# A 32-byte shift of the left-side pools, spread row pitches for split weights, and one value buffer less, in an encoder layer on one core

## The chip, the cores and the metric

The kernel runs on one NeuronCore of a Trainium2 chip. The metric is the device time of one launch in microseconds, the median of the runs shown.

## The reference

One layer of an encoder is computed for two sequences of 1024 tokens with a model width of 1024. Each sequence has its own conditioning vector, from which six shifts, scales and gates are made. An input projection feeds a latent attention with four heads and, beside it, a Fourier mixing; one output projection joins them. Behind it stands a SwiGLU feed-forward of width 2816. All values are float32.

```python
h2 = rmsnorm(x, g_ffn) * (1.0 + sc2) + sh2
ffn = (jax.nn.silu(h2 @ w_gate) * (h2 @ w_up)) @ w_down
return x + ga2 * ffn          # then a final rmsnorm with g_final
```

The change touches the feed-forward alone, and by its shift of addresses all that lies on the left side of the on-chip memory.

## The kernel before

**Split products.** A float32 product is made of three matmuls in the type float32r. `split(hi, lo, src)` makes two tiles: ScalarE casts src to hi (line 62) and VectorE subtracts hi from src to make lo (line 63). `mm3(out, lh, ll, rh, rl, ...)` then issues three matmuls of 128x512 on TensorE (lines 78, 79 and 80): lh with rh, lh with rl, ll with rh. In each, the operand that is loaded into the array comes first, and the one that streams through it second.

**Block products.** Each large product of the feed-forward (gate and up, then down) is done with seven products of half-size blocks instead of eight, on sums and differences of blocks. The sums and differences are formed by `sums_w`, `comb_h`, `down_combos` and `put_s`, mostly on GpSimd (lines 134 and 137 are the helpers `sub` and `add`).

**Gate and up.** For each sequence s the loop runs over 22 column blocks of the two weight matrices. The seven combinations of the hidden input, H[k], are held on chip for the whole loop as split pairs of tiles (128 partitions, four chunks of 512). The weights of a block come by DMA into `rgu` (line 1205), are combined, and each of the seven results (128 by 512) is split by `hl` into a tile wh and a tile wl. `prod(ps, k, wt, first)` goes over four chunks c: it loads columns 128c to 128c+127 of wh or wl into the array and streams chunk c of H[k] through it, twelve matmuls for a product. `step(j, ...)` calls prod and then splits the j-th weight of the next block. VectorE and ScalarE take the seven results out of PSUM and form the blocks that GpSimd and SP store to `s_d`.

**Down.** For each sequence seven calls of `prod2` follow: k = 0, 5, 1, 6, 4, 3, 2, into the PSUM banks X, Y, X, Y, Z, Y, Z. Each goes over eleven blocks f. A block's two raw operands are loaded on SP's queue into `draw` (lines 1397 and 1398), which has two buffers of two blocks each; both operands are split by `hl`, and twelve matmuls follow, in which 128 columns of the first operand (ah, al) are loaded and all 512 columns of the second (bh, bl) stream. Between the blocks `hooks` works through a list of small tasks. `resid` loads a piece of the residual into a value buffer (line 1411, SP's queue), multiplies by the gate on VectorE (line 1412) and adds on GpSimd; `first_squares` writes squares into a scratch value buffer on ScalarE (line 1422); `last_part` and `rows_out` finish rows and store them. In the last sequence the seventh product is replaced by a loop over operands that are kept as H tiles (`held`).

**Buffers.** `val()` gives one of VALS value buffers of 128x512, `hl` one of eight wh and one of eight wl buffers. A buffer is given again when its last reader is done; the instruction that writes it first waits for that, and what stands behind it in its engine's or queue's order waits too. The order of instructions on each engine is made by a scheduler from the order of the program text and from these buffers.

**Places.** On-chip memory is filled by pools from two sides. The pool const is the first on the left. Among the left-side tiles are H, rgu, draw and the attention's latents; wh, wl, val, the tables of the projection and the probabilities lie on the right side.

Of the kernel before, what the change touches and what calls it, by code (L numbers as in the profile page):

```python
# [12 lines left out]
F32 = mybir.dt.float32  # L13
F32R = mybir.dt.float32r
# [7 lines left out]
P = 128  # L22
# [10 lines left out]
G = 8  # L33
GD = 64
NOUT = 6
VALS = 18
FF = 2816
NF = FF // P
EPS = 1e-6
# [13 lines left out]
def hybrid_encoder_kernel(ctx: ExitStack, tc: tile.TileContext, a: dict):  # L53
# [7 lines left out]
    def split(hi, lo, src):  # L61
        here["a"] = nc.scalar.copy(hi, src).ins  # L62
        here["v"] = nc.vector.tensor_tensor(out=lo, in0=src, in1=rd(hi), op=ALU.subtract).ins  # L63
# [13 lines left out]
    def mm3(out, lh, ll, rh, rl, first, last, cont=False):  # L77
        nc.tensor.matmul(out, lh, rh, start=first, stop=False, skip_group_check=cont)  # L78
        nc.tensor.matmul(out, lh, rl, start=False, stop=False, skip_group_check=cont)  # L79
        nc.tensor.matmul(out, ll, rh, start=False, stop=last, skip_group_check=cont)  # L80

    const = ctx.enter_context(tc.tile_pool(name="const", bufs=1))
# [7 lines left out]
    mhalf = const.tile([P, 2], F32, name="mhalf")  # L90
    nc.gpsimd.memset(mhalf, -0.5)
    cmask = const.tile([P, 7], F32, name="cmask")
    nc.sync.dma_start(cmask, a["cmask"])

    def rstd(ms, n, rest=None):
# [755 lines left out]
    with ExitStack() as st:  # L851
# [145 lines left out]
        for k in range(nit + 4):  # L997
# [7 lines left out]
            if k < nit:  # L1005
                s, b, h, u = items[k]
# [28 lines left out]
    with ExitStack() as st:  # L1035
# [95 lines left out]
        H = {}  # L1131
# [42 lines left out]
        w5 = st.enter_context(tc.tile_pool(name="p5b", bufs=1, side="right", reuse_waits="tile"))  # L1174
# [5 lines left out]
        def val():  # L1180
            return w5.tile([P, 512], F32, tag="v", name="val", bufs=VALS)

        def hl(v):
            h = w5.tile([P, 512], F32R, tag="wh", name="wh", bufs=8)
            if "gf" not in S:
                S["gf"] = w5.tile([P, D], F32, name="gf")
                w5.tile([P, 2, 512], F32, tag="ga", name="tdb", bufs=1)
            l = w5.tile([P, 512], F32R, tag="wl", name="wl", bufs=8)
            split(h, l, v)
            return h, l  # L1190

# [3 lines left out]
        for s in range(2):  # L1195
# [44 lines left out]
            def prod(ps, k, wt, first):  # L1240
                wh, wl = wt
                for c in range(4):
                    cs = slice(c * P, c * P + P)
                    mm3(ps, wh[:, cs], wl[:, cs], H[k][0][:, c, :], H[k][1][:, c, :], first and c == 0, c == 3, not first)

            def store_s(k, fi, v, eng):
                eng.dma_start(s_d[s][k, fi], v)
# [18 lines left out]
            if s == 0:  # L1266
                wts = [hl(w0[i]) for i in range(2)]
                next(prep, None)
                wts += [hl(w0[i]) for i in (2, 3)]
            else:  # L1270
                wts = first_w
            A = {}
            late = None
            for n, f in enumerate(order):
# [10 lines left out]
                def step(j, ps, k, first, src=src):  # L1285
                    prod(ps, k, cur[j], first)
                    if s == 0 and n == 0:
                        if j == 0:
                            cur.extend(hl(v) for v in w0[4:])
                            w0.clear()  # L1290
                            norm3(1, S.pop("jk3").bitcast(BF16))
                        if j < 3:
                            with behind():
                                for _ in range(2):
                                    next(prep, None)
                            return
                        if j == 3:
                            src = S["w1"] = sums_w(src, lambda i: val(), nc.vector)
                        src = S["w1"]
                        for i in ((), (), (), (0, 1), (2, 3), (4,), (5, 6))[j]:  # L1300
                            nxt.append(hl(src[i]))
                    elif src is not None:
                        nxt.append(hl(src[j]))
                    if s == 0 and n == 1 and j == 2:
                        S.pop("w1", None)
                        flip2(3, [S.pop(("xn", 1, 3, u)) for u in range(2)], bank, lambda g: val())
# [80 lines left out]
            def bsrc(k, f):  # L1387
                r1 = slice(f * P, f * P + P)
                r2 = slice((f + NF // 2) * P, (f + NF // 2) * P + P)
                return {0: wd[r1, :512], 1: wd[r2, :512], 2: wd[r2, 512:], 3: t_d[0, f], 4: t_d[1, f], 5: t_d[2, f], 6: t_d[3, f]}[k]  # L1390

            def prod2(ps, k, first, last, hook=None):
                for f in range(NF // 2):
                    if f % 2 == 0:
                        raw2 = w.tile([P, 2, 2, 512], F32, tag=f"X{f // 2 % 2}", name="draw", bufs=1)
                    raw = raw2[:, f % 2]
                    nc.sync.dma_start(raw[:, 0, :], s_d[s][k, f])  # L1397
                    nc.sync.dma_start(raw[:, 1, :], bsrc(k, f))  # L1398
                    ah, al = hl(raw[:, 0, :])
                    bh, bl = hl(raw[:, 1, :])  # L1400
                    for t in range(4):
                        tt = slice(t * P, t * P + P)
                        mm3(ps[t], ah[:, tt], al[:, tt], bh, bl, first and f == 0, last and f == NF // 2 - 1, not first)
                    if hook is not None:
                        hook(f)
# [61 lines left out]
            X = [bank() for _ in range(4)]  # L1467
            Y = [bank() for _ in range(4)]
            prod2(X, 0, True, True)
            p1 = [val() for _ in range(4)]  # L1470
            for t in range(4):
                nc.scalar.copy(p1[t], X[t])
            prod2(Y, 5, True, True, put_next)
            u2 = [val() for _ in range(4)]
            for t in range(4):
                add(u2[t], Y[t], p1[t], nc.vector)
            prod2(X, 1, False, True, put_next)
            c11 = [val() for _ in range(4)]
            for t in range(4):
# [51 lines left out]
            H = Hn  # L1531
# [99 lines left out]
```

## Time and profile before

| | |
|---|---|
| median of 2 runs | 2116.02 us (2114.76 to 2117.27) |
| span of the profiled execution | 2109.8 us |
| mean granted TensorE clock in it | 0.988 |
| TensorE busy | 2033.0 us (96%) |
| VectorE, ScalarE, GpSimd busy | 1414.4, 906.0, 828.6 us |
| DMA | 371.30 MB, mean 176 GB/s |

The span reaches from the first to the last instruction on the core. The time of a run also holds what lies around it: 6.2 us, if the profiled execution is set against the median of the runs. In the profile's rows PE is TensorE's matmuls, PEld its loads, DVE VectorE, ACT ScalarE, POOL GpSimd, and SPq the queue of SP, which issues most DMAs. A row of a group has the line, the engine, the operation, what is written and read, the shape and count; then the busy time in us and the mean of one in ns; then the idle time just before these instructions and what ended it. A row of a window has the stretch and its length, then for PE, PEld, DVE, ACT and POOL the busy time with the count, then the granted clock, the busy share of the DMA engines and GB/s. A row of waits has the total, the number of times and the longest, in us. A row of the timeline has the start and the duration in us.

### The profile page before, as it was taken

To read this page: it belongs to the slowest core of one execution; us is meant where nothing else is said; L and a number is where in the kernel's file an instruction comes from. 1 tells how busy PE (TensorE), PEld (TensorE's weight loads), DVE (VectorE), ACT (ScalarE), POOL (GpSimd) and SP (SyncE) were. 2 spreads that over 40 slices of the span, in tenths; PEclk is the share of its full clock that TensorE was granted. 3 is DMA by queue.
4 is the path that set the end of the run, shared out by engine and by line. 5 is a ranking of instruction groups with operands and counts; after the bars stand their busy time and mean duration, and the time that the engine had idled before them with its cause. 6 is when DMAs were issued, how large, how long until landed. Compare 5 with 4: busy or idle time off the path is not lost. (4 is left out here: it accounts for less than half of the span.)

```text
span 2109.8 us, 28784 instructions
## 1 busy us (share of the span) xinstructions
PE 2033.0 (96%) x10044; PEld 1667.0 (79%) x10044; DVE 1414.4 (67%) x2087; ACT 906.0 (43%) x1763; POOL 828.6 (39%) x1018
## 2 busy tenths in 40 slices
PE   5899998999999999999999999999999999999998
PEld 2788876888888887788888888887788888888886
DVE  2657756766676678777677677777766666566685
ACT  2656534555565555232333346453233333336441
POOL 1455202111311314888778610235544454420142
PEclk8999999999999999999999999999999999999999
DMA  9575765544544455554554578674332232247772
GB/s 368 194 248 190 248 233 197 113 88 91 159 119 118 150 186 211 180 193 169 194 185 166 174 250 270 222 236 164 131 119 90 91 125 95 81 154 280 233 227 99
DMA packets 184254, 371.30 MB, mean 176 GB/s; under 512 B 19052, under 2 KB 58604, under 8 KB 181036
## 3 DMA queue, kind: packets, MB, share of 16 engines
q1 hardware_dynamic: 166252, 314.00, 44.1%
q0 software_dynamic: 17856, 55.45, 8.9%
q8 instruction: 79, 1.29, 0.2%
q14 instruction: 67, 0.55, 0.1%
HBM read 257.38 MB, written 120.39 MB: 179 GB/s over the span
## 5 line engine op out<-in xcount | busy, mean ns | idle before, releaser
L78 PE MATMUL bank<-H,wh 128*128 128x512 f32 x1232 | 489.6, 398 | 7.7 <-ACT val L1311 4.0
L80 PE MATMUL bank<-H,wl 128*128 128x512 f32 x1232 | 488.9, 397 | 1.4 <-DVE wl L63 1.4
L79 PE MATMUL bank<-H,wh 128*128 128x512 f32 x1232 | 489.0, 397 | 0.0
L137 DVE TENSOR_TENSOR val<-bank,val 128x512 f32<-128x512 f32 x244 | 167.1, 690 | 185.7 <-PE bank L80 178.6
L78 PEld LDWEIGHTS bank<-H,wh 128*128 128x128 f32 x1232 | 232.5, 189 | 66.8 <-ACT val L1311 5.4
L80 PEld LDWEIGHTS bank<-H,wl 128*128 128x128 f32 x1232 | 232.5, 189 | 57.9 <-DVE wl L63 1.7
L79 PEld LDWEIGHTS bank<-H,wh 128*128 128x128 f32 x1232 | 232.7, 189 | 56.2
L63 DVE TENSOR_TENSOR wl<-draw,wh 128x512 fp32r<-128x512 f32 x286 | 203.1, 744 | 82.7 <-ACT wh L62 80.7
L62 ACT CAST wh<-draw 128x512 fp32r<-128x512 f32 x286 | 168.8, 619 | 159.0 <-PE bank L79 83.0
L137 POOL TENSOR_TENSOR val<-val 128x512 f32<-128x512 f32 x58 | 82.9, 1438 | 366.3 <-DVE val L1412 187.6
L79 PE MATMUL bank<-wl,wh 128*128 128x512 f32 x572 | 223.8, 391 | 1.6 <-DVE wl L63 1.6
L80 PE MATMUL bank<-wh,wl 128*128 128x512 f32 x572 | 222.7, 389 | 0.0
L78 PE MATMUL bank<-wh 128*128 128x512 f32 x572 | 222.6, 389 | 0.0
L62 ACT CAST wh<-rgu 128x512 fp32r<-128x512 f32 x172 | 106.7, 621 | 269.7 <-PE bank L79 209.5
L62 ACT CAST wh<-val 128x512 fp32r<-128x512 f32 x133 | 82.2, 622 | 280.5 <-PE bank L79 249.1
L63 DVE TENSOR_TENSOR wl<-val,wh 128x512 fp32r<-128x512 f32 x133 | 141.5, 1066 | 85.6 <-ACT wh L62 85.5
L63 DVE TENSOR_TENSOR wl<-rgu,wh 128x512 fp32r<-128x512 f32 x172 | 169.4, 985 | 4.9 <-ACT wh L62 4.8
L134 POOL TENSOR_TENSOR val<-rgu 128x512 f32<-128x512 f32 x84 | 122.8, 1462 | 125.0 <-DMA rgu<-in_wgu_dram 108.8
L79 PEld LDWEIGHTS bank<-wl,wh 128*128 128x128 f32 x572 | 107.4, 188 | 27.3 <-DVE wl L63 5.3
L78 PEld LDWEIGHTS bank<-wh 128*128 128x128 f32 x572 | 107.4, 188 | 22.4
L80 PEld LDWEIGHTS bank<-wh,wl 128*128 128x128 f32 x572 | 107.4, 188 | 22.0
L134 POOL TENSOR_TENSOR val<-val 128x512 f32<-128x512 f32 x89 | 119.4, 1357 | 1.3
(332 smaller groups left out, 4051.2 us busy)
## 6 DMA issues: line engine op xcount, KB each, us to landing
rgu<-in_wgu_dram SPq DMA_DIRECT2D x86, 512.0 KB
draw<-s_d SPq DMA_DIRECT2D x143, 256.0 KB
s_d<-val POOLq DMA_DIRECT2D x88, 256.0 KB, 4.1
draw<-t_d SPq DMA_DIRECT2D x88, 256.0 KB
s_d<-val SPq DMA_DIRECT2D x66, 256.0 KB
draw<-in_w_down_dram SPq DMA_DIRECT2D x55, 256.0 KB
wada<-in_w_ada_dram SPq DMA_DIRECT2D x13, 1024.0 KB
xt<-in_x_dram SPq DMA_DIRECT2D x16, 512.0 KB
```

The lines of the kernel that those rows point to most:

```text
L62: here["a"] = nc.scalar.copy(hi, src).ins
L63: here["v"] = nc.vector.tensor_tensor(out=lo, in0=src, in1=rd(hi), op=ALU.subtract).ins
L78: nc.tensor.matmul(out, lh, rh, start=first, stop=False, skip_group_check=cont)
L79: nc.tensor.matmul(out, lh, rl, start=False, stop=False, skip_group_check=cont)
L80: nc.tensor.matmul(out, ll, rh, start=False, stop=last, skip_group_check=cont)
L134: return eng.tensor_tensor(out=out, in0=x, in1=y, op=ALU.subtract).ins
L137: eng.tensor_tensor(out=out, in0=x, in1=y, op=ALU.add)
```

## The change

A tile of 8 float32 values (32 bytes in each partition) that nothing uses is added to the pool const, so that everything allocated later on the left side lies 32 bytes higher. The tiles wh and wl get room for four rows of 132 and of 134 elements (528 and 536 bytes) in place of 512 elements, and in gate and up the four chunks of 128 columns are written to and loaded from these rows. In down, `hl` is called with flat=True and uses the first 512 elements without gaps, in the same larger buffers. VALS goes from 18 to 17. The lines behind the new tile move by one in the new file, those behind the new code by four.

```diff
-VALS = 18
+VALS = 17
...
     cmask = const.tile([P, 7], F32, name="cmask")
+    const.tile([P, 8], F32, name="phase")
...
-        def hl(v):
-            h = w5.tile([P, 512], F32R, tag="wh", name="wh", bufs=8)
+        def hl(v, flat=False):
+            h = w5.tile([P, 4, 132], F32R, tag="wh", name="wh", bufs=8)
             if "gf" not in S:
                 S["gf"] = w5.tile([P, D], F32, name="gf")
                 w5.tile([P, 2, 512], F32, tag="ga", name="tdb", bufs=1)
-            l = w5.tile([P, 512], F32R, tag="wl", name="wl", bufs=8)
+            l = w5.tile([P, 4, 134], F32R, tag="wl", name="wl", bufs=8)
+            if flat:
+                h, l = (t.rearrange("p a b -> p (a b)")[:, :512] for t in (h, l))
+            else:
+                h, l, v = h[:, :, :128], l[:, :, :128], v.rearrange("p (a b) -> p a b", a=4)
             split(h, l, v)
             return h, l
...
                 for c in range(4):
-                    cs = slice(c * P, c * P + P)
-                    mm3(ps, wh[:, cs], wl[:, cs], H[k][0][:, c, :], H[k][1][:, c, :], first and c == 0, c == 3, not first)
+                    mm3(ps, wh[:, c, :], wl[:, c, :], H[k][0][:, c, :], H[k][1][:, c, :], first and c == 0, c == 3, not first)
...
-                    ah, al = hl(raw[:, 0, :])
-                    bh, bl = hl(raw[:, 1, :])
+                    ah, al = hl(raw[:, 0, :], True)
+                    bh, bl = hl(raw[:, 1, :], True)
```

## The prediction

> **What bounds the kernel now.** I read the page first, for the busy shares:
>
> ```profile
> span 2109.8 us, 28784 instructions
> PE 2033.0 (96%) x10044; PEld 1667.0 (79%) x10044; DVE 1414.4 (67%) x2087; ACT 906.0 (43%) x1763; POOL 828.6 (39%) x1018
> ```
>
> TensorE is busy for 96% of the span, so a gain must come from the pace at which matmuls follow each other, or from its last waits. The groups by line show which matmuls these are, and that they are not equally quick:
>
> ```profile
> L78 PE MATMUL bank<-H,wh 128*128 128x512 f32 x1232 | 489.6, 398 | 7.7 <-ACT val L1311 4.0 <-DVE val L137 3.4 <-ACT wh L62 0.2
> L79 PE MATMUL bank<-H,wh 128*128 128x512 f32 x1232 | 489.0, 397 | 0.0
> L80 PE MATMUL bank<-H,wl 128*128 128x512 f32 x1232 | 488.9, 397 | 1.4 <-DVE wl L63 1.4
> L80 PE MATMUL bank<-wh,wl 128*128 128x512 f32 x572 | 222.7, 389 | 0.0
> L78 PE MATMUL bank<-wh 128*128 128x512 f32 x572 | 222.6, 389 | 0.0
> L78 PE MATMUL bank<-H 128*128 128x512 f32 x44 | 17.1, 389 | 0.0
> ```
>
> The same 128x512 product costs 397 ns with H moving and wh or wl loaded (the gate/up stage, 3696 of them), 389 ns in the down stage (1716), and 389 ns with H moving and H loaded. These are durations of pipelined instructions; the pace is a count over a stretch. The windows are, in order: gate/up of sequence 0, gate/up of sequence 1, two stretches of down, and the last products, where both operands are H tiles.
>
> ```profile
> 1000.00:1140.00 140.00, 140.00 (x601) 112.70 (x601) 98.43 (x101) 43.01 (x72) 108.38 (x100) 1.00 0.52 179
> 1560.00:1830.00 270.00, 270.00 (x1159) 217.37 (x1158) 169.01 (x192) 81.95 (x138) 130.63 (x112) 1.00 0.28 98
> 1240.00:1380.00 140.00, 140.00 (x620) 115.95 (x619) 103.85 (x148) 75.89 (x138) 24.59 (x22) 1.00 0.78 259
> 1960.00:2030.00 70.00, 70.00 (x311) 57.97 (x310) 48.28 (x66) 30.55 (x57) 19.25 (x16) 1.00 0.68 222
> 2072.00:2095.00 23.00, 23.00 (x103) 19.02 (x103) 14.37 (x23) 2.90 (x8) 10.20 (x35) 1.00 0.35 129
> ```
>
> A window counts each matmul that it touches, 1.7 more than it starts (0.39 us over the pace). So the paces are 140/599.3 = 233.6 and 270/1157.3 = 233.3 ns in gate/up, 140/618.3 = 226.4 and 70/309.3 = 226.3 ns in down, and 23/101.3 = 227.0 ns in the last products. The granted clock is 1.00 in all five. Load elsewhere does not explain the 7 ns: GpSimd is busy 77% in the first row and 48% in the second, at one pace, and the down rows carry more DMA (0.78, 0.68) than the slow ones (0.52, 0.28). What goes with it is where the operands lie. In the built program H lies at 0 modulo 64 bytes and wh and wl at 32, so moving and loaded operand differ by 32. In down both are wh or wl (both 32), and in the last products both are H (both 0): offset 0. The waits of TensorE in these stages are small:
>
> ```profile
> PE bank L78 <- ACT val L1311: 4.0, 2, 2.6
> PE bank L78 <- DVE val L137: 3.4, 3, 2.1
> PE bank L79 <- DVE wl L63: 1.6, 3, 1.0
> PE bank L80 <- DVE wl L63: 1.4, 1, 1.4
> ```
>
> 10.4 us of waiting in 1300: pace is the bound, and the feeding chains are just in time.
>
> **The change, part by part.** No matmul is added or removed; the built programs have the same TensorE order. What changes is addresses and one buffer.
>
> *Gate/up.* H moves to 32 modulo 64. With rows of 528 bytes, the four 128-column chunks of a wh tile start 0, 16, 32 and 48 bytes from H; those of wl, at 536 bytes, 0, 24, 48 and 8, or 32, 56, 16 and 40 in every second buffer, since a wl buffer of 2144 bytes is 33.5 times 64. So the shift alone would give offset 0 everywhere, and the pitches spread the offsets again. Nothing in the trace runs at these offsets in full; the nearest is the stage of wm, where operands lie at 0, 8, 32 and 40 from each other in turn. From its first to its last row here are 35 intervals:
>
> ```profile
> 317.77 0.39 PE L80 MATMUL bank<-wm,A 128*128 128x512 f32 x1
> ...
> 325.90 0.40 PE L78 MATMUL bank<-wm,B 128*128 128x512 f32 x1
> ```
>
> 8.13/35 = 232.3 ns: a mixture is nearly as slow as 32 throughout. I take 232.3 against 233.4 as the mean of the two gate/up stages: -1.1 x 3696 = -4 us. Bounds: every pair at the down pace, -7 x 3696 = -26 us; a second step of the same size up, +26 us. If the whole fixed cost of a load beside a stream went away, the gain would be larger. That cost comes from the 256-wide products:
>
> ```profile
> 340.53 0.28 PE L80 MATMUL gb<-ql,wq_l 128*128 128x256 f32 x1
> ...
> 341.59 0.28 PE L80 MATMUL gb<-wq_h,ql 128*128 128x256 f32 x1
> ```
>
> Nine intervals give 117.8 ns; 2 x (226.4 - 117.8) = 217.2 ns is the streaming of 512 columns, and 233.4 - 217.2 = 16.2 ns x 3696 = 60 us is the floor. The Trainium skill, "TensorE: Matmul & The Clock Gate", Back-to-back issue gap, has about 216 ns for 512 columns alone, by which it would be 64 us.
>
> *Attention.* The latents are left-side tiles and also move by 32. Half of their 640 products now run at offset 32 and come to 0, as the mean of these rows, between 389 and 397, bears out:
>
> ```profile
> L906 PE MATMUL ps_s<-lat,qp 128*128 128x512 f32 x128 | 50.6, 396 | 0.0
> L907 PE MATMUL ps_s<-lat,qp 128*128 128x512 f32 x128 | 50.6, 395 | 0.0
> L79 PE MATMUL gb<-pt,ckv 128*128 128x256 f32 x256 | 72.7, 284 | 0.0
> L79 PE MATMUL gb<-ql,wq_h 128*128 128x256 f32 x64 | 18.3, 286 | 0.0
> ```
>
> 320 x 7 = 2.2, taken as -2 us (0 to -4.5). The 768 products of pt with ckv go the other way, from 32 to 0, where the ql row is 2 ns longer: +1 us (-1.5 to +4).
>
> *Down.* Here hl is asked for flat tiles, so no chunk is spread, but the wl buffers still alternate between 0 and 32. A pair of calls takes neighbouring buffers, so al and bl now always differ by 32. Of each three products (ah with bh, ah with bl, al with bh) the one that streams bl while al is loaded has offset 32. If that one alone pays: 572 x 7 = +4 us; all three: 1716 x 7 = +12; none: 0. I take +5, since the next product starts later too.
>
> *The splits.* Cast and subtraction now write four runs of 128 with a gap. The nearest row is L873, which writes four runs of 64:
>
> ```profile
> L873 DVE TENSOR_TENSOR qsk<-qt,qsk 128x256 fp32r<-128x256 f32 x16 | 8.9, 559 | 1.8 <-ACT qsk L872 1.1
> L867 DVE TENSOR_TENSOR qt<-gb,rc 128x256 f32<-128x256 f32 x16 | 6.6, 415 | 1.1 <-PE gb L80 1.1
> L63 DVE TENSOR_TENSOR wl<-rgu,wh 128x512 fp32r<-128x512 f32 x172 | 169.4, 985 | 4.9 <-ACT wh L62 4.8
> ```
>
> At worst 559/415 = 1.35 times 985 ns, 0.35 us more per twelve products (2.8 us). VectorE is busy 70% and 63% in the gate/up windows, and would reach 82%: hidden, 0. Without that cover it would be 305 x 0.35 = 107 us.
>
> *Seventeen value buffers.* The order of instructions stays the same on all engines but around the fifth and sixth product of down (Z with k = 4, Y with k = 3), so only there do values run out: p1, u2, c11 and u3 hold sixteen, and the residual loads (L1411) and the scratch of the squares (L1422) share the rest: two before, one after. A load waits in SP's queue for a free buffer, and the draw loads behind it wait too. Before, two loads are in flight and the additions that free them come in pairs:
>
> ```profile
> 2007.49 3.21 SPq L1411 DMA_DIRECT2D val<-x_d  x2
> ...
> 2020.87 0.82 SPq L1411 DMA_DIRECT2D val<-x_d  x2
> 2021.79 0.37 SPq L1397 DMA_DIRECT2D draw<-s_d  x1
> 2022.21 0.43 SPq L1398 DMA_DIRECT2D draw<-t_d  x1
> 2025.06 2.02 SPq L1411 DMA_DIRECT2D val<-x_d  x2
> ```
>
> ```profile
> 2011.86 3.52 POOL L137 TENSOR_TENSOR val<-val 128x512 f32<-128x512 f32 x2 [1.06 <-DMA val<-x_d]
> 2023.59 3.15 POOL L137 TENSOR_TENSOR val<-val 128x512 f32<-128x512 f32 x2 [1.44 <-DMA val<-x_d]
> 2050.56 1.61 POOL L137 TENSOR_TENSOR val<-val 128x512 f32<-128x512 f32 x1
> ```
>
> Alone, one load takes 2.7 us (2020.87 to 2023.59) and 1.6 us of addition, 4.4 with the issue. Twelve such and eight squares of 0.9 make 60 us, where 2007.5 to 2052.2 was 45. The two products last 22 x 12 x 226.4 ns = 60 us, so it just fits; but the last draw loads are some 16 us later in the queue, and the row of L79 above says TensorE already waits for wl a little. The changed order puts several draw loads ahead of the residual loads, which gives part of it back. I take 4 us for each sequence, +8; bounds 0, and 24 each, +48.
>
> **Sum.** -4 - 2 + 1 + 5 + 0 + 8 = +8 us, on a span of 2109.8. The median of the runs is 2116.02, 6.2 above the span, so the forecast is 2109.8 + 8 + 6.2 = 2124 us: no change by 2%, which is 42 us and about what a measurement of this kernel can tell from none.
>
> **Rivals.**
> *A, the offsets lock at the quick pace.* Gate/up runs at 226.4, since short runs of each offset pay only once: -26, and with -2, +1, 0 in down and +2 for buffers 2091 us. For it: offset 0 now occurs among the others. Against: wm.
> *B, the spread takes the fixed cost away.* -60 - 2 + 1 + 5 + 8 = -48, 2068 us. For it: 32 bytes matter, so finer steps may. Against: no row of 512 columns runs below 226.
> *C, slower: SP's queue.* Each residual load holds the draws behind it until its predecessor's buffer is free, and TensorE runs dry when the chain's 16 us exceed the lead of the draws, with more behind the casts: +24 for each sequence, other terms at their sum of 0, 2164 us. For it: the waits above. Against: the draws put forward.
> *D, addresses do not set the pace*, and the change does not do what it is laid out for: 0 for all address terms, +8 or less, 2116 to 2124 us. The five windows speak against it. The Trainium skill, same page, What happens when you issue a matmul (Step-by-step), gives TensorE two independent read ports, for the streamed and for the loaded operand, by which D would hold; the trace, with 233.4 beside 226.4 ns at one clock, does not agree.
>
> **How the numbers follow.** Forecast (2108 to 2140) 0.54, A 0.17, B 0.08, C 0.10, D 0.11. The range reaches down past A, to 2084, and up to 2150, half way to C; it leaves out B and the worse half of C. Faster than 2074 is B: 0.08. Slower than 2158 is C where it is full: 0.07. The rest, 0.85, is within 2%.
>
> **What would show it.** Windows of gate/up: about 602 matmuls in 140 us as now (A: 620, B: 645). Down: the row of L79 longer than L78 and L80, 392 to 396 instead of 389. Waits: "val<-x_d" loads one at a time, L79 or L78 waiting for wl some 4 us around each Z and Y product. It is wrong if gate/up moves by more than 3 ns per product in either direction, or if TensorE waits over 15 us there.

## The result: 1.1% slower, and the profile after

The changed kernel takes 2138.82 us (2137.44 to 2140.2) against 2116.02 before: a ratio of 1.011, 95% interval 1.0094 to 1.0126. That is 22.8 us more, inside the range given, and slower as forecast, but 15 us above the forecast of 2124. The head of the page:

```profile
span 2135.7 us, 28734 instructions
PE 2043.0 (96%) x10044; PEld 1672.7 (78%) x10044; DVE 1391.6 (65%) x2087; ACT 904.8 (42%) x1763; POOL 822.1 (38%) x1018
```

TensorE's share of busy time is the same 96%. The windows, in the order in which they were shown for the kernel before (gate/up twice, down twice):

```profile
1000.00:1140.00 140.00, 140.00 (x605) 113.22 (x604) 99.36 (x100) 42.41 (x72) 109.90 (x99) 1.00 0.52 176
1560.00:1830.00 270.00, 270.00 (x1166) 218.82 (x1165) 159.24 (x194) 82.89 (x139) 132.23 (x111) 1.00 0.28 100
1240.00:1380.00 140.00, 140.00 (x606) 113.43 (x605) 100.90 (x148) 75.94 (x138) 19.15 (x18) 1.00 0.77 258
1960.00:2030.00 70.00, 70.00 (x304) 56.76 (x303) 45.92 (x67) 30.72 (x54) 7.67 (x5) 1.00 0.66 216
```

With the same 1.7 taken off each count, gate/up runs at 140/603.3 = 232.1 and 270/1164.3 = 231.9 ns (before: 233.6 and 233.3), and down at 140/604.3 = 231.7 and 70/302.3 = 231.6 ns (before: 226.4 and 226.3). Down has lost its quick pace. The groups by line, with the attention's:

```profile
L79 PE MATMUL bank<-wl,wh 128*128 128x512 f32 x572 | 228.8, 400 | 5.2 <-DVE wl L63 5.1
L78 PE MATMUL bank<-wh 128*128 128x512 f32 x572 | 227.2, 397 | 7.8 <-ACT wh L62 7.8
L80 PE MATMUL bank<-wh,wl 128*128 128x512 f32 x572 | 226.9, 397 | 0.0
L79 PE MATMUL gb<-pt,ckv 128*128 128x256 f32 x256 | 73.3, 286 | 0.0
L907 PE MATMUL ps_s<-lat,qp 128*128 128x512 f32 x128 | 50.7, 396 | 0.0
L908 PE MATMUL ps_s<-lat,qp 128*128 128x512 f32 x128 | 50.4, 393 | 0.0
```

All three products of down pay, not only L79's. And TensorE waits where it did not (the view of waits):

```profile
PE bank L78 <- ACT wh L62: 8.1, 5, 2.4
PE bank L79 <- DVE wl L63: 5.1, 7, 2.3
```

That is 13.2 us for split operands against 1.6 before. A wait can cost more than its own length. TensorE's timeline in down of sequence 0, around the longest one:

```profile
1409.96 0.40 PE L80 MATMUL bank<-wh,wl 128*128 128x512 f32 x1
1412.11 0.50 PE L78 MATMUL bank<-wh 128*128 128x512 f32 x1 [1.76 <-ACT wh L62]
...
1413.78 0.63 PE L79 MATMUL bank<-wl,wh 128*128 128x512 f32 x1
...
1416.76 0.45 PE L80 MATMUL bank<-wh,wl 128*128 128x512 f32 x1
1417.05 0.40 PE L78 MATMUL bank<-wh 128*128 128x512 f32 x1
```

From 1413.78 to 1416.76 the products start 2.98/7 = 0.426 us apart instead of 0.232. From 1412.11 to 1417.05 there are twelve intervals, 4.94 us in place of 2.8: a wait of 1.8 us has brought another 2.1 us behind it. The granted clock of the stretch from 1408 to 1420 is 0.86, and that of the slow products alone 0.50:

```profile
1413.70:1416.70 3.00, 3.00 (x8) 2.34 (x7) 0.69 (x1) 0.62 (x1) 1.25 (x1) 0.50 0.53 193
```

Not every wait does this. Behind one of 2.2 us that ends at 1521.0 in the same trace the products soon start 0.23 us apart, and the granted clock from 1521 to 1526 is 1.00. The Trainium skill, "TensorE: Matmul & The Clock Gate", What's actually happening, has a half-rate clock after an idle window of about 3.4 us. In this trace the half rate stands behind 1.8 us of idleness. The Trainium skill, same page, "Wait — 56ns, not 53.3ns?", has 426.7 ns for 512 columns at that rate. The trace agrees, with 0.426 us.

### The profile page after: what moved, and what is told of

It reads as the page before. It is cut to its first block, busy times and chain, and to the rows that moved or that the text cites. A ratio compares the mean times of both kernels' runs of the same rounds, so it can differ in the third digit from the quotient of the medians.

```text
span 2135.7 us, 28734 instructions
## 1 busy us (share of the span) xinstructions
PE 2043.0 (96%) x10044; PEld 1672.7 (78%) x10044; DVE 1391.6 (65%) x2087; ACT 904.8 (42%) x1763; POOL 822.1 (38%) x1018
## 4 chain that ended last, share of the span: by engine, by line
PE 50%; DMA 4%; POOL 3%; DVE 2%; issue 2%; ACT 1%; SPq 0%; POOLq 0%; ACTq 0%; DVEq 0%
PE bank L78 17%; PE bank L79 17%; PE bank L80 17%; DMA val<-x_d 2%; POOL val L138 1%; DVE wl L63 1%; DMA rgu<-in_wgu_dram 1%; DVE val L138 0%; DMA draw<-s_d 0%; POOL val L135 0%; DMA draw<-in_w_down_dram 0%; ACT wh L62 0%; POOL rs_y L106 0%; DVE val L1442 0%; DVE H L63 0%
## 5 line engine op out<-in xcount | busy, mean ns | idle before, releaser
L78 PE MATMUL bank<-H,wh 128*128 128x512 f32 x1232 | 488.9, 397 | 9.7 <-ACT val L1315 6.1
L79 PE MATMUL bank<-H,wh 128*128 128x512 f32 x1232 | 487.1, 395 | 0.0
L138 DVE TENSOR_TENSOR val<-bank,val 128x512 f32<-128x512 f32 x244 | 166.9, 689 | 199.0 <-PE bank L80 196.7
L78 PEld LDWEIGHTS bank<-H,wh 128*128 128x128 f32 x1232 | 232.6, 189 | 67.3 <-ACT val L1315 7.4
L79 PEld LDWEIGHTS bank<-H,wh 128*128 128x128 f32 x1232 | 233.0, 189 | 54.1
L63 DVE TENSOR_TENSOR wl<-draw,wh 128x512 fp32r<-128x512 f32 x286 | 198.2, 726 | 114.0 <-ACT wh L62 113.5
L138 POOL TENSOR_TENSOR val<-val 128x512 f32<-128x512 f32 x58 | 80.6, 1392 | 445.6 <-DVE val L1416 169.6
L78 PE MATMUL bank<-wh 128*128 128x512 f32 x572 | 227.2, 397 | 7.8 <-ACT wh L62 7.8
L79 PE MATMUL bank<-wl,wh 128*128 128x512 f32 x572 | 228.8, 400 | 5.2 <-DVE wl L63 5.1
L63 DVE TENSOR_TENSOR wl<-rgu,wh 128x512 fp32r<-128x512 f32 x172 | 150.1, 873 | 6.8 <-ACT wh L62 6.7
L78 PEld LDWEIGHTS bank<-wh 128*128 128x128 f32 x572 | 108.5, 190 | 35.4 <-ACT wh L62 9.6
L79 PEld LDWEIGHTS bank<-wl,wh 128*128 128x128 f32 x572 | 108.6, 190 | 33.7 <-DVE wl L63 8.8
```

The source lines that it names most:

```text
L138: eng.tensor_tensor(out=out, in0=x, in1=y, op=ALU.add)
```

## The experiments

Two questions were open: what the missing buffer costs and by which road, and what sets the pace of the products. All ratios are against the kernel before, run beside it, with 95% intervals. A kernel's time can be set against its own neighbour only, since the kernel before took 2115.0 to 2116.4 us beside them.

**One part alone: the buffer, and the shift.**

```diff
-VALS = 18
+VALS = 17
```

> The kernel before with seventeen value buffers, nothing else. Theory T (the loss of the change is the missing buffer: residual loads wait one at a time in SP's queue, draws and casts behind them come late, and TensorE pays the stall and some ten slow products behind it): down of both sequences has about 17 us more of stalls, its undisturbed pace stays 226-227 ns, so 2116 + 17 = 2133 us (2127 to 2138). Rival A (the predicted size, stalls without the slow products behind them): +8, 2124 us. Rival B (the stalls of the changed kernel come from its slower down products and strided tiles, not from the buffer): 2116 us.

Measured: 2133.44 against 2114.98 us, ratio 1.0097 (1.0076 to 1.0117): +18.5 us, theory T. Its waits of TensorE, and its down windows:

```profile
PE bank L79 <- DVE wl L63: 8.7, 10, 2.3
PE bank L78 <- ACT wh L62: 8.4, 4, 3.0
```

```profile
1240.00:1380.00 140.00, 140.00 (x620) 115.96 (x619) 100.50 (x149) 75.47 (x138) 17.24 (x17) 1.00 0.75 253
```

17.1 us of waiting against 1.6, while the pace between them is the old one: 620 matmuls in 140 us. So buffer and pace are separate losses.

```diff
     cmask = const.tile([P, 7], F32, name="cmask")
+    const.tile([P, 8], F32, name="phase")
```

> The kernel before with the 32-byte tile alone: flat wh and wl, eighteen value buffers. Streamed H and loaded wh or wl then lie at one offset modulo 64 throughout gate/up. Theory T (the distance of loaded and streamed operand sets the pace; a steady distance of 0 runs at 226.7 ns): 6.7 x 3696 = -25 us, attention -2, pt with ckv +1, in all 2090 us (2086 to 2096), with about 618 matmuls in 140 us of gate/up. Rival A (the quick pace of down has another reason than the distance, for instance that H comes from a left-side pool): 2114 to 2118 us and about 601 matmuls. Rival B (TensorE gains but then waits for wh and wl, whose chain is just in time): 2096 to 2112 us with waits of L78 and L79 over 20 us.

Measured: 2096.22 us, ratio 0.9913 (0.9898 to 0.9927). A gate/up window of this kernel, and its waits:

```profile
1560.00:1830.00 270.00, 270.00 (x1193) 223.61 (x1192) 158.94 (x199) 84.40 (x142) 133.93 (x112) 1.00 0.29 103
```

```profile
PE bank L78 <- DVE val L138: 5.5, 4, 2.9
PE bank L79 <- DVE wl L63: 3.7, 4, 1.4
```

270/1191.3 = 226.6 ns where it was 233.3: moving the left-side tiles by 32 bytes, the streamed H among them, and nothing else gives gate/up the pace of down. The 6.7 ns on 3696 products are the 25 us expected. The time came out 0.2 us above theory T's range, and some of the gain is given back in waits (L79 for wl 3.7 us against 1.6, L78 for val 5.5 against 3.4). By its time alone it lies in rival B's range too, but the waits of over 20 us on L78 and L79 that B named did not come; these are some 14 us.

**The period of the distance.** The prediction counted distances modulo 64 bytes. A wl buffer of 2144 bytes is 32 past a multiple of 64, and this I made responsible for down.

```diff
-            l = w5.tile([P, 4, 134], F32R, tag="wl", name="wl", bufs=8)
+            l = w5.tile([P, 544], F32R, tag="wl", name="wl", bufs=8)[:, :536].rearrange("p (a b) -> p a b", a=4)
```

> The changed kernel with wl buffers of 544 instead of 536 elements (2176 bytes, 34 times 64), rows as before at 536 bytes: al and bl of down lie at one distance again. Theory T (the slower down pace of the changed kernel, 231.8 against 226.9 ns over some 1700 products, is the distance of 32 between neighbouring wl buffers, and all three products of a triple pay): undisturbed down pace back at 227 ns, -8 us, stalls as in the changed kernel, gate/up within 3 us: 2131 us (2127 to 2135). Rival (the slower down pace is a consequence of the stalls or of the splits): 2139 us, pace 231 to 232.

Measured: 2137.6 us, 1.0114 (1.0099 to 1.0129), and down no quicker:

```profile
1240.00:1380.00 140.00, 140.00 (x606) 113.49 (x605) 100.69 (x149) 75.07 (x136) 16.58 (x17) 1.00 0.75 252
```

606 matmuls, as in the changed kernel. All distances of down are now multiples of 64 (wh buffers of 2112 bytes are 64 past a multiple of 256, these wl buffers 128 past one). So either the period is not 64, or distances that change from product to product cost by themselves. Three kernels hold the distance in gate/up steady at other multiples of 64; a fourth makes the distances of down multiples of 128.

```diff
-    const.tile([P, 8], F32, name="phase")
+    const.tile([P, 24], F32, name="phase")
```

> The kernel before with a tile of 96 instead of 32 bytes ahead of the left-side pools, flat wh and wl, eighteen value buffers: H and wh or wl lie 64 bytes apart throughout gate/up, a distance that is 0 modulo 64 but not modulo 128. Theory P64 (the pace goes by the distance modulo 64; the 231.8 ns that stayed in down when al and bl were made equal modulo 64 comes from distances that change from product to product): gate/up at 226.8 ns, 2096 us (2092 to 2100). Theory P128 (it goes by the distance modulo 128 or more): gate/up stays at 233 ns, 2115 us (2111 to 2119).

```diff
-            h = w5.tile([P, 4, 132], F32R, tag="wh", name="wh", bufs=8)
+            h = w5.tile([P, 544], F32R, tag="wh", name="wh", bufs=8)[:, :528].rearrange("p (a b) -> p a b", a=4)
```

> The changed kernel with both wh and wl buffers at 2176 bytes (17 times 128), rows as before at 528 and 536: all operands of down lie at distances of 0 or 128 modulo 256. Theory P128: undisturbed down pace back at 227 ns, -8 us on 2138: 2130 us (2126 to 2134). Theory P64, by which the changing distances cost, or a period of 256 and more: down stays at 231 to 232 ns, 2138 us. The stalls of down (some 20 us) stay in both.

```diff
-    const.tile([P, 8], F32, name="phase")
+    const.tile([P, 40], F32, name="phase")
```

> The kernel before with 160 bytes ahead of the left-side pools: H and wh or wl lie 128 bytes apart throughout gate/up, flat tiles, eighteen value buffers. Theory P512 (only a distance that is 0 modulo 512, or nearly, is quick; 64 gave 228.9 ns): gate/up at 228 to 233 ns, 2099 to 2115 us. Theory P128 (distances of 0 modulo 128 are quick, and what keeps down at 231 ns in the changed kernel with 2176-byte buffers is that its distances change): gate/up at 226.8 ns, 2096 us (2092 to 2099).

```diff
-    const.tile([P, 8], F32, name="phase")
+    const.tile([P, 72], F32, name="phase")
```

> The same with 288 bytes: 256 bytes between H and wh or wl. Theory P512: gate/up at 228 to 233 ns, 2099 to 2115 us. Theories P128 and P256 (quick at 0 modulo 128, or 256): 226.8 ns, 2096 us (2092 to 2099).

Measured: 64 bytes apart 2098.7 us, 0.9927 (0.9906 to 0.9947); 128 apart 2115.07 us, 0.9999 (0.9987 to 1.0011); 256 apart 2093.18 us, 0.9904 (0.9877 to 0.993); down at multiples of 128 2138.02 us, 1.0102 (1.0077 to 1.0128). The gate/up windows at 64, at 128 and at 256 bytes:

```profile
1560.00:1830.00 270.00, 270.00 (x1181) 221.52 (x1181) 158.28 (x197) 83.50 (x140) 135.46 (x112) 1.00 0.29 103
```

```profile
1560.00:1830.00 270.00, 270.00 (x1163) 218.92 (x1162) 161.43 (x193) 82.24 (x138) 134.92 (x112) 1.00 0.29 103
```

```profile
1560.00:1830.00 270.00, 270.00 (x1193) 223.65 (x1192) 158.97 (x200) 84.86 (x142) 134.03 (x112) 1.00 0.29 103
```

And the down window of the kernel whose buffers are both 2176 bytes:

```profile
1240.00:1380.00 140.00, 140.00 (x609) 114.02 (x608) 101.98 (x151) 75.46 (x138) 17.28 (x18) 1.00 0.76 257
```

Together, at a granted clock of 1.00:

| distance of streamed and loaded operand | pace |
|---|---|
| 0 (gate/up with the shift) | 270/1191.3 = 226.6 ns |
| 32, the streamed one below (gate/up before) | 233.3 ns |
| 64, the streamed one above | 270/1179.3 = 228.9 ns |
| 128 | 270/1161.3 = 232.5 ns |
| 256 | 270/1191.3 = 226.6 ns |

These five steady distances fit a period of 256 bytes: 256 is as quick as 0, and 128 is nearly as slow as 32. P64, P128 and P512 fell; P256, named beside P128 in one expectation only, fits all five. The time at 64 bytes, 2098.7 us, lies inside P64's range; it is the slow pace at 128 that speaks against P64, and the quick one at 256 against P512. The pace at 64 is a mean. By line its products differ, though all of them lie 64 bytes apart modulo 256:

```profile
L78 PE MATMUL bank<-H,wh 128*128 128x512 f32 x1232 | 481.6, 391 | 9.2 <-ACT val L1312 4.8 <-DVE val L138 3.8 <-ACT wh L62 0.2
L79 PE MATMUL bank<-H,wh 128*128 128x512 f32 x1232 | 484.5, 393 | 0.0
L80 PE MATMUL bank<-H,wl 128*128 128x512 f32 x1232 | 486.9, 395 | 1.4 <-DVE wl L63 1.4
```

So more than this distance plays in. Down of the changed kernel fits in its direction: wh buffers of 2112 bytes and wl buffers of 2144 put the operands of neighbouring buffers 64 and 96 bytes apart modulo 256, so none of its three products is at 0. Its amount is not explained. With two products of three at the 228.9 ns of 64, the third would have to take 3 x 231.7 - 2 x 228.9 = 237.3 ns, more than any row of the table. In the built program the streamed operand of those two lies mostly 64 below the loaded one, not above as in the table, and the distances change from block to block; neither was tried by itself. With both buffers at 2176 the distance is 128 for most products, and the pace 140/607.3 = 230.5 ns. The few products of that stage that lie at 0 among them (71 by the built program) are followed by the next after 230.8 ns in its trace, no sooner than the others. What was seen to be quick is therefore a distance that stays at 0.

The rule also holds for these 128x512 products only. The 256-wide products of pt with ckv lie 32 bytes apart before and have 284 to 286 ns by their three rows; at 0, in the changed kernel, they have 286 to 289, and at 64 the other way, in the kernel with the tile of 96 bytes, 282 to 285. There 0 is slower than 32. Why the places cost what they do, why 64 costs less than 32, was not tried.

**The road from the missing buffer to TensorE.** First, the residual loads on GpSimd's queue in the changed kernel.

```diff
-                nc.sync.dma_start(xr, x2_d[s][r0 : r0 + P, gs])
+                nc.gpsimd.dma_start(xr, x2_d[s][r0 : r0 + P, gs])
```

> The changed kernel with the residual loads (L1415) issued by GpSimd, which also does the additions that free their buffers, instead of SP. Theory T (a residual load that waits for a buffer holds the draw loads behind it in SP's queue): the draws come in time, down's stalls fall by 10 to 17 us, 2122 to 2129 us. Rival A (the additions and squares that free the buffers set the time, whichever queue waits): 2136 to 2142 us, with GpSimd now the engine named in the waits. Rival B (GpSimd is held up by its own waiting loads and delivers values later): above 2142 us.

Measured: 2161.56 us, 1.0226 (1.0211 to 1.0242): theory T missed, rival B came true. TensorE's waits, and ScalarE's between 1350 and 1440:

```profile
PE bank L78 <- ACT wh L62: 33.7, 2, 17.8
```

```profile
ACT val L1426 <- POOL val L138: 32.3, 4, 20.6
```

The draws were no longer behind the loads, but ScalarE's squares (L1426) waited up to 20.6 us for GpSimd's additions, and the casts behind them in ScalarE's order came late. SP's queue is only one half of the road; the squares are the other. The next two give loads or squares a place of their own.

```diff
-VALS = 18
+VALS = 17
...
-                xr = val()
+                xr = w5.tile([P, 512], F32, tag="xr", name="xr", bufs=1)
```

> The kernel before with seventeen value buffers and one buffer of its own for the residual loads: eighteen in all, as before, but only one residual load can be in flight, and the squares keep the seventeenth value buffer. Theory T (what costs is that residual loads go one at a time in SP's queue with the draws behind them): down's stalls stay near those of seventeen buffers, 2126 to 2133 us. Rival (what costs is the total, residual loads and squares sharing one buffer): stalls as before, 2113 to 2120 us.

Measured: 2118.08 against 2116.40 us, 1.0015 (1.0001 to 1.0029). Theory T fell: one load at a time costs hardly anything. In the kernel before, the loss of a buffer shows only when loads and squares share the last one. ScalarE's waits between 1350 and 1425, in this kernel and then in the one with seventeen buffers alone:

```profile
ACT wh L62 <- DMA draw<-s_d: 14.9, 9, 2.9
ACT val L1422 <- POOL val L137: 2.0, 1, 2.0
```

```profile
ACT wh L62 <- DMA draw<-s_d: 15.8, 6, 7.3
ACT val L1422 <- POOL val L137: 12.3, 4, 4.2
```

The waits for draws are of the same total, but the longest is 7.3 us instead of 2.9, and the squares wait 12.3 instead of 2.0 us. The squares' waits alone are not the sign of a loss, since they are 8.6 us in the kernel before as well, where the longest wait for a draw is 3.7 us:

```profile
ACT wh L62 <- DMA draw<-s_d: 14.5, 9, 3.7
ACT val L1422 <- POOL val L137: 8.6, 2, 4.7
```

This bears out a loop: a load waits in SP's queue for the buffer that a square will use first; the square stands in ScalarE's order behind casts; the casts wait for draws that stand in SP's queue behind the load. It can be followed in the kernel with seventeen buffers alone, on ScalarE and then in SP's queue (rows between these are left out):

```profile
1374.51 0.63 ACT L1422 ACTIVATE val<-val 128x512 f32<-128x512 f32 x1 [3.74 <-POOL val L137]
1379.46 0.63 ACT L1422 ACTIVATE val<-val 128x512 f32<-128x512 f32 x1 [2.15 <-POOL val L137]
1407.05 1.95 ACT L62 CAST wh<-draw 128x512 fp32r<-128x512 f32 x3 [7.34 <-DMA draw<-s_d]
```

```profile
1375.26 5.26 SPq L1411 DMA_DIRECT2D val<-x_d  x2
1380.69 0.32 SPq L1397 DMA_DIRECT2D draw<-s_d  x1
1397.42 5.03 SPq L1411 DMA_DIRECT2D val<-x_d  x2
1402.54 0.38 SPq L1397 DMA_DIRECT2D draw<-s_d  x1
```

A square waits 3.7 us for an addition and ends at 1375.1; only then, at 1375.26, does a residual load go. The load behind it is through at 1380.5, after the square of 1379.46 has ended, and the next draw goes at 1380.69. No draw is issued between 1397.4 and 1402.5 either, and ScalarE's longest wait, to 1407.05, is for a draw behind that. No square stands in the way there, only one load behind another; with a buffer of their own such a pair takes 4.5 us too, without so long a wait. That the squares before had used up the lead of the draws is an argument, not a measurement. Then the squares' own tile in the changed kernel itself:

```diff
-                jk = val()
+                jk = w5.tile([P, 512], BF16, tag="jk", name="jk", bufs=1)
```

> The changed kernel with a small tile of its own (512 bf16 columns) for the discarded output of the squares, so that the seventeenth value buffer serves the residual loads alone. Theory L (the loop costs: a load waits for the buffer that a square holds, the square stands in ScalarE's order behind casts, the casts wait for draws that stand in SP's queue behind the load): the stalls of down fall from 21 us to 4 to 8, and what is left of the change is its addresses, 2119 to 2125 us. Rival (the stalls of the changed kernel are also its slower down products and its splits): 2130 us or more. Addresses stay: down at 231 to 232 ns, gate/up at 232.

Measured: 2126.16 us, 1.0057 (1.004 to 1.0073), just above theory L's range. In down alone these waits shrink from 12.9 to 6.6 us:

```profile
PE bank L78 <- ACT wh L62: 3.5, 2, 2.2
PE bank L79 <- DVE wl L63: 3.1, 5, 1.4
```

So the loop is some (1.011 - 1.0057) x 2116 = 11 us of the changed kernel's loss. What is left, 10.9 us (2126.16 against 2115.30), is more than the addresses' 4 us (next section). Of these waits 6.6 us remain against 1.6 before, which makes up 5 us of the rest; whether the single load or the slower pace keeps them was not settled.

**More buffers, or less need of them.** Both start from the shift alone.

```diff
-VALS = 18
+VALS = 20
...
-            h = w5.tile([P, 512], F32R, tag="wh", name="wh", bufs=8)
+            h = w5.tile([P, 512], F32R, tag="wh", name="wh", bufs=7)
...
-            l = w5.tile([P, 512], F32R, tag="wl", name="wl", bufs=8)
+            l = w5.tile([P, 512], F32R, tag="wl", name="wl", bufs=7)
```

> The 32-byte tile alone, with seven instead of eight wh and wl buffers and twenty instead of eighteen value buffers in the same room. Theory: the residual loads and squares of down get four buffers instead of two, so draws come earlier and the stalls of down and gate/up (25 us with eighteen) shrink by 3 to 8: 2090 us (2086 to 2094). Rival (the eighth pair of split tiles is what keeps TensorE fed): L78 and L79 wait for wh and wl, 2098 to 2115 us.

Measured: 2102.63 us, 0.994 (0.9918 to 0.9962), slower than the shift alone, by the rival: TensorE waits for split tiles,

```profile
PE bank L79 <- DVE wl L63: 4.6, 8, 1.3
PE bank L78 <- ACT wh L62: 3.9, 4, 2.3
```

In down this is 8.5 us against 3.7 with eight of each. It is not all: the waits of L78 there for VectorE's additions out of PSUM (L138) rose as well, from 3.2 to 6.5 us.

```diff
-                jk = val()
-                nc.scalar.activation(jk, v, AF.Square, scale=1.0 / 32.0, accum_out=m[half, t][:, 0:1])
+                jk = w5.tile([P, 512], mybir.dt.float8e4, tag="jk", name="jk", bufs=1)
+                nc.scalar.activation(jk, v, AF.Square, scale=1.0 / 32.0, accum_out=m[half, t][:, 0:1], saturate=False)
```

> The 32-byte tile alone with eighteen value buffers, and a tile of 512 bytes (8-bit floats) for the discarded output of the squares, which then takes no value buffer. Theory L: residual loads have two buffers to themselves and the stalls of down (5.7 us with the 32-byte tile alone) fall to 2 to 4: 2093 us (2090 to 2096), below both kernels. Rival (what is left of down's stalls has another cause): 2096 us, as without it.

Measured: 2093.65 us, 0.9907 (0.989 to 0.9925). The time lies in theory L's range, but the rival is only 2.4 us away and inside what these runs can tell. L79 waits 1.6 us for wl in down, as before the change, against 3.7 with the shift alone:

```profile
PE bank L79 <- DVE wl L63: 1.6, 3, 1.0
```

Three versions thus lie 0.9% below the kernel before and about 2% below the changed one: the shift by 32 bytes, by 288, and by 32 with the squares' small tile. Their intervals overlap, so none of the three is shown to be best.

## Why the prediction was right, and where its steps were not

The direction, the size (no change by the measure of 2%) and the range held, by a sum of which two terms were too small, one of them for a wrong reason:

| term | forecast | measured |
|---|---|---|
| gate/up | -4 | (232.0 - 233.4) x 3696 = -5 us |
| attention, lat and pt | -1 | about 0 (lat 396 and 393 ns, before 396 and 395; pt with ckv 286, before 284) |
| down | +5 | (231.7 - 226.4) x 1716 = +9 us |
| splits | 0 | 0 |
| seventeen buffers | +8 | +18.5 us alone |
| sum | +8 | +22.5 (22.8 measured) |

By its sum the forecast was off by nearly a factor of three, +8 against +22.8, with both misses on the same side; the range held because it reached half way to rival C. That the measured terms meet the total within 0.3 us is closer than an interval of some 3 us either way can show, and the 18.5 us come from another kernel. In the changed kernel itself the waits for split operands rose by 11.6 us (13.2 against 1.6), and slow products stand behind some of them. The waits stayed under the 15 us that the prediction named as a sign of being wrong; in the kernel with seventeen buffers alone they are 17.1. The 6.2 us between span and time are mostly a difference between executions: where both are known for one run they are 1.7 us apart (2137.44 and 2135.7 in the changed kernel).

*Gate/up.* The window was to hold about 602 matmuls, and holds 605. The step stood on the mixture of the wm stage and held; that the shift alone would give distance 0 throughout was borne out with it. The ground was counted modulo 64, though. That 32 bytes also bring the distance to 0 modulo 256 is luck: in the built program before, H lies at 192 and wh and wl at 224 modulo 256. That the pitches take this gain back is what the change does to gate/up: 226.6 ns with the shift, 231.9 with the pitches.

*Down, the step that failed by its mechanism.* That only one product of three would lie away from 0 came from counting modulo 64. Rows of before could have told. In the built program the products of the wm stage with B lie at 0 modulo 64 throughout, 64 modulo 256, and these start 1.15/5 = 230 ns apart, not 226.4:

```profile
318.24 0.40 PE L78 MATMUL bank<-wm,B 128*128 128x512 f32 x1
...
319.39 0.40 PE L80 MATMUL bank<-wm,B 128*128 128x512 f32 x1
```

Counted modulo 256, all three products of down are away from 0, and all three pay. The upper bound given, +12, was a little nearer to the +9 than the +5 taken. L79's row was to be longer than the others, 392 to 396 beside 389; it is 400, and the others rose to 397 as well.

*Splits.* They were allowed at worst 1.35 times their duration. They became shorter:

```profile
L63 DVE TENSOR_TENSOR wl<-rgu,wh 128x512 fp32r<-128x512 f32 x172 | 150.1, 873 | 6.8 <-ACT wh L62 6.7
```

873 ns against 985. Writing with gaps costs nothing here, and no gain of it is shown either: the same row has 945 ns with the shift alone, without gaps, and 936 in the kernel with wider wl buffers, with gaps.

*Seventeen buffers, the term that was mis-sized.* The place (down's Z and Y products), the one-at-a-time loads and the waits for wl were as described, but 4 us for each sequence were 9. The working chained loads, additions and squares one behind another, 60 us against 60 us of products, and left out two things: that a square stands behind casts which wait for draws behind the next load, so that the chain is a loop with TensorE's feed in it, and that TensorE can run at half pace for some 3 us behind a wait of about 2 us.

*Rivals.* A and B are out (605 matmuls, not 620 or 645). C had the right mechanism and too high a price (24 us for each sequence). D is out by the shift alone: 32 bytes moved 18.8 us. The Trainium skill, "TensorE: Matmul & The Clock Gate", Step-by-step: what each phase is for, has two independent read ports, by which loading takes no read bandwidth from the running matmul. These runs do not bear out that the places of the two operands are then of no account: a shift of the streamed one by 32 bytes changes the pace by 6.7 ns, and the measurement decides.

## What to carry to other kernels

Where matmuls stand back to back with a load for each, look at the place of the streamed and of the loaded operand modulo 256 bytes in the built program, and measure: one 32-byte tile was worth 0.9% here for 512-wide products, while 256-wide ones did not gain, and a padding of buffers that is no multiple of 256 cost 5 ns on each product of another stage. A padding by a whole multiple of 256 was not tried. When a pool loses a buffer, write down who shares the last one: two users that stand in different queues, each behind something the other needs, make a loop, and a small tile for a discarded output opens it. Cost a wait of TensorE at somewhat more than its length: with seventeen buffers alone 15.5 us more of waiting cost 18.5 us, while the one followed above cost twice its length.

## What was not expected of the hardware

The pace of a 128x512 product with a load beside it goes by the operands' distance where that is steady, and five distances fit a period of 256 bytes: 226.6 ns at 0 and 256, 228.9 (a mean of three unlike products) at 64, 232.5 at 128, 233.3 at 32. The mixed distances of the changed gate/up give 231.9 to 232.1. The 256-wide products of pt with ckv do not follow this: 284 to 286 ns at 32, 286 to 289 at 0. Behind an idle time of 1.8 us the products started 0.426 us apart for about 3 us, at a granted clock of 0.50; behind one of 2.2 us none did.
